# Sums of weight blocks in a seven-product up-projection: on VectorE, or by accumulating DMAs

## The chip, the core and the metric

One core of a Trainium2 chip runs the whole program. The metric is the time of one execution on the device in microseconds (us). Of the two versions the same input is computed in one launch.

## What is computed

One decoder layer over 512 tokens of width 2048, in float32: two mixer branches, an output projection, and then the part that the change is in, a gated feed-forward block of width 5632.

```python
h = rms_norm(x, ffn_norm_g[l])
gate, up = jnp.split(h @ w_up[l], 2, axis=-1)
gate = causal_depthwise_conv(gate, ffn_conv_w[l]) + ffn_conv_b[l]
x = x + (jax.nn.silu(gate) * up) @ w_down[l]
...
return rms_norm(x, final_norm_g)
```

## The kernel before

**Stages.** The program runs the mixers, the output projection, the up-projection and the down-projection one after the other on TensorE. Every float32 product is three matmuls: each operand is split into a high and a low part of type float32r, and `mm3` (line 486) adds high times high, high times low and low times high in PSUM. ScalarE casts the high part of a weight piece (`ACT.copy`), VectorE subtracts it from the raw weights and gets the low part. All instructions are recorded by one helper, so the profile gives line 97 (L97) for nearly all; tiles tell them apart.

**The up-projection.** The loop over `f` (lines 491 to 522) has 44 pairs: 128 columns of gate and 128 columns of up. The weights of a pair are four blocks of 128 x 1024 (512 KB each): block `ij` has i = 1 for gate and 2 for up, j = 1 or 2 for the two halves of the 2048 input channels. The tokens also come in two halves of 256. Eight block products would be due; a scheme of the Strassen-Winograd kind makes seven. Each is 8 steps of 3 matmuls of 256 columns, so a pair has 168 matmuls. Four of the seven weight operands are sums of blocks. The operands of the tokens, `XB` (plain halves) and `XT` (sums and differences), are made once, in `operands` (line 1272), from `h`, the tokens scaled by `ffn_g`. PSUM banks `bx`, `by`, `bz`, `bv` take the seven products, and `up_out` (line 1423) adds them up on VectorE, applies `rstd2`, the convolution, silu and the product, and stores the result to `scr_a`.

**The weights' path.** `up_products` (line 1333) is a generator that `refill` (line 1415) advances between matmuls until 6 pieces are ready ahead of TensorE. Before, SP loads blocks 11 and 22 into `raw` (3 buffers) and blocks 12 and 21 into `uraw` (3 buffers). `cast` (line 1355) makes the high part of half a block on ScalarE, `low` (line 1364) the low part on VectorE. The pieces live in two rings of 4 high and 4 low buffers (`whi`/`wlo` and `uhi`/`ulo`), so at most 8 pieces exist. `combine` (line 1369) is one VectorE instruction over 128 x 1024; `steps` (line 1375) lists the seven operands in the order in which they are made and hangs four `combine`s and the next pair's loads on them, as actions after the first or second cast of an operand. Blocks are overwritten in place: 22 becomes 22 + 21, and so on.

**Order of the work.** Every engine carries out its own instructions in program order. That order comes from `Flow` (line 102), a planner that keeps a clock for each engine (`account`, line 145) and decides between which matmuls the other engines' instructions are emitted. SP issues all loads and stores in one queue; a load that waits for its buffer holds up what is behind it. GpSimd has no work in the up-projection but one small power operation at its start (`rsqrt_pow`, line 437, called by `rms_rows`, line 577, for `rstd2`).

**The start of the stage.** The first three blocks of pair 0 (11, 22, 12) are loaded by the general plan, `up_at` in `plan_all` (line 536); block 21 of pair 0 is loaded at the first call of `up_products`.

Of the kernel before, what the change touches and what calls it, by code (L numbers as in the profile page):

```python
# [13 lines left out]
F32 = mybir.dt.float32  # L14
# [26 lines left out]
]  # L41
KH = KT // 2
PAIRS = [m for j in range(KH) for m in (j, j + KH)]
D_PRE, D_LEFT, D_RIGHT = 8, 38, 24
SPLIT_TILES = 1
BA_LAG = 3
# [55 lines left out]
class Flow:  # L102
# [42 lines left out]
    def account(self, eng, op, out, ins, kw):  # L145
        c = self.clock
        ko, ki = self.key(out), [self.key(i) for i in ins]
        start = c[eng]
        for k in ki if op == "dma_start" else ki + [ko]:
            r, e = self.ready.get(k, (0.0, None))  # L150
            start = max(start, r + self.SEM * (not (e == eng == "pe")) + 0.05 * (e == "pe" != eng))
        start = max(start, self.avail.get(ko, 0.0) + self.SEM)
        if op == "dma_start":
            size = out.nbytes if hasattr(out, "nbytes") else 0
            size = int(np.prod(out.shape)) * 4
            if eng == "pool":
                c["pool"] = go = start + 1.08
            else:
                c[eng] = start
                c["hw"] = go = max(start, c["hw"]) + 0.45  # L160
            run = size / 360e3 * (2.0 if int(out.shape[-1]) * 4 < 512 else 1.0)
            c["dma"] = max(go + 0.65, c["dma"]) + run
            end = c["dma"] + 1.0
        else:
            n = int(np.prod(out.shape[1:]))
            ni = max([n] + [int(np.prod(i.shape[1:])) for i in ins]) if op in ("tensor_reduce", "bn_stats") else n
            if eng == "pe":
                rhs = kw.get("rhs", kw.get("identity"))
                cols = int(np.prod(rhs.shape[1:]))
                floor = 0.025  # L170
                if op == "transpose":
                    rate = 2
                elif rhs.dtype == F32:
                    rate, floor = 4, int(np.prod(kw["lhsT"].shape[1:])) / 600.0
                else:
                    rate, floor = 1, (cols + 32) / 2400.0
                dur = max(cols * rate / 2400.0, floor) + (0.0025 if rate > 1 else 0.0)
                if start - c["pe"] > 0.05:
                    self.stall += start - c["pe"]
                    self.log.append((round(c["pe"], 1), round(start - c["pe"], 2), str(ko)))  # L180
            elif eng == "act":
                ps = any(k.split("_")[0] in PSUM_NAMES for k in ki if isinstance(k, str))
                aps = sum(hasattr(kw.get(a), "tensor") for a in ("scale", "bias"))
                dur = n / 1200.0 + (0.051 if ps else 0.093) + 0.093 * aps
                f = kw.get("func")
                if f in (AF.Silu, AF.Exp, AF.Sigmoid) and f != self.table:
                    self.table = f
                    dur += 1.28
            elif eng == "dve":
                ap_scalar = op == "scalar_tensor_tensor" or hasattr(kw.get("scalar1"), "tensor")  # L190
                dur = (ni + (124 if ap_scalar else 66)) / 960.0
            else:
                dur = 0.96 if kw.get("op") == ALU.pow else n * (0.0009 if op == "memset" else 0.002) + 0.03
            end = c[eng] = start + dur
        self.ready[ko] = (end, eng if op != "dma_start" else None)
        for k in ki + [ko]:
            self.last[k] = max(self.last.get(k, 0.0), end)
# [107 lines left out]
def tile_trunk(ctx: ExitStack, tc: tile.TileContext, xT, w_k, w_ba, w_m, pw, w_out, w_up, w_down, par_d, cst_d, out):  # L305
# [97 lines left out]
    def pc(n, i=0, w=1):  # L403
        return par[:, OFF[n] - KT + i : OFF[n] - KT + i + w]
# [187 lines left out]
            fl.matmul(ps2[:, blk(i)], lhsT=r[:, i : i + 1].to_broadcast([P, P]), rhs=ident)  # L592
        return r, ps2

    def rms_stats(total, bcast):
        r, ps2 = yield from rms_rows([total], range(NB))
        ACT.copy(out=bcast, in_=ps2)
        free(ps2)
        return r

# [659 lines left out]

    xpool = xctx.enter_context(tc.tile_pool(name="operands", bufs=1, reuse_waits="tile"))
    tpool = tctx.enter_context(tc.tile_pool(name="halves", bufs=1, side="right", reuse_waits="tile"))
    XT = [fl.tile(xpool, [P, 4, T], F32R, "xt", KH, nm("xt")) for _ in range(KH)]
# [6 lines left out]
    def operands(j, xa, xb):  # L1272
        h = fl.tile(tpool, [P, 2 * T], F32, "h", 2, nm("h"))
        for i, x in enumerate((xa, xb)):
            ACT.activation(out=h[:, i * T : (i + 1) * T], in_=x, func=AF.Copy, scale=pc("ffn_g", j + i * KH))
        fl.live["xv"] -= 2
        yield S(h)
        d = fl.tile(tpool, [P, 2 * T], F32, "d", 2, nm("d"))
# [1 line left out]
        ACT.copy(out=b[:, 0, 0:HT], in_=h[:, 0:HT])  # L1280
        ACT.copy(out=b[:, 1:3, 0:HT], in_=v2(h[:, T:]))
        V.tensor_tensor(
            out=v2(d[:, 0:T]), in0=h.rearrange("p (a b) -> p a b", b=T)[:, :, HT:T], in1=v2(h[:, 0:T]),
            op=ALU.subtract)
        yield S(b)
        V.tensor_tensor(out=b[:, 0, HT:T], in0=h[:, 0:HT], in1=b[:, 0, 0:HT].bitcast(F32), op=ALU.subtract)
        V.tensor_tensor(out=d[:, T : T + HT], in0=h[:, T + HT :], in1=d[:, 0:HT], op=ALU.subtract)
        V.tensor_tensor(out=b[:, 1:3, HT:T], in0=v2(h[:, T:]), in1=b[:, 1:3, 0:HT].bitcast(F32), op=ALU.subtract)
        V.tensor_tensor(out=d[:, T + HT :], in0=h[:, T : T + HT], in1=d[:, T : T + HT], op=ALU.subtract)
        yield S(d)  # L1290
        ACT.copy(out=xt[:, :, 0:HT], in_=v2(d))
        yield S(xt)
        V.tensor_tensor(out=xt[:, :, HT:T], in0=v2(d), in1=xt[:, :, 0:HT].bitcast(F32), op=ALU.subtract)

    xvs = []

    def load_xv():
# [22 lines left out]
            op_ev.append(fl.spawn(operands(i // 2, xvs[i - 1], t)))  # L1320
    rstd2 = rstd_tile("rstd2_bc")
    fl.drain(op_ev)
    fl.spawn(rms_stats(total, rstd2))
    tctx.close()
    actx.close()
    dpre = ctx.enter_context(tc.tile_pool(name="down0", bufs=1, side="right", reuse_waits="tile"))
# [6 lines left out]
    def up_products():  # L1333


        blocks = {}

        def load(f, *names):
            for n in names:
                if f == NF:  # L1340
                    if n in (11, 22):
                        up_done.append(True)
                        load_next()
                    continue
                i, j = n // 10 - 1, n % 10 - 1
                if n in (11, 22):
                    t = fl.tile(wpool, [P, 1024], F32, "raw", 3, nm("wraw"))
                else:
                    t = U("uraw", 3, 1024)
                SP.dma_start(t, w_up[2 * f + i][:, j * 1024 : (j + 1) * 1024])  # L1350
                blocks[f, n] = t

        pend = deque()

# [11 lines left out]
            V.tensor_tensor(out=lo, in0=src, in1=hi.bitcast(F32), op=ALU.subtract)  # L1366
            pieces.append((hi, lo))

        def combine(out, a, b, op=ALU.subtract):
            V.tensor_tensor(out=out, in0=a, in1=b, op=op)  # L1370

        blocks.update({(0, n): raws[up_at + i] for i, n in enumerate((11, 22, 12))})
        load(0, 21)

        def steps(f, a11, a22, a12, a21):

            def start():
                load(f + 1, 21)
                if f:
                    load(f + 1, 11)  # L1380

            def s2():
                combine(a22, a22, a11)
                load(f + 1, 22 if f else 11)

            return [
                (a11, start, None), (a22, None, lambda: combine(a22, a21, a22, ALU.add)),
                (a12, lambda: combine(a21, a11, a21), None), (a22, None, s2),
                (a21, lambda: combine(a12, a12, a22), lambda: load(f + 1, 12)),
                (a22, None, None if f else lambda: load(1, 22)), (a12, None, None)]  # L1390

        then = None
        for f in range(NF):
            units = steps(f, *[blocks.pop((f, n)) for n in (11, 22, 12, 21)])
            if f == 0:
                units[0][1]()
                units[1][2]()
                yield
                units = units[2:]
            for t, *acts in units:  # L1400
# [90 lines left out]
    for f in range(NF):  # L1491
# [2 lines left out]
        ev2, ev3, ev4 = Event(), Event(), Event()  # L1494
        if f == NF - 1:
            early = fl.spawn(act_loads(range(D_PRE // 2)))
        for n, (b, c, x) in enumerate((
                (bx, 0, [t[:, 0] for t in XB]), (bz, HT, [t[:, 3] for t in XT]), (bv, 0, [t[:, 1] for t in XB]),
                (by, 0, [t[:, 0] for t in XT]), (by, HT, [t[:, 1] for t in XT]), (bx, HT, [t[:, 2] for t in XT]),
                (bz, 0, [t[:, 2] for t in XB]))):  # L1500
            for k in range(KH):
                if k % 4 == 0:
                    hi, lo = pieces.popleft()
# [6 lines left out]
                if k % 4 == 3:  # L1510
                    for _ in step:
                        pass
            if n == 0:
                s1 = U("s1", 2, HT)
                ACT.copy(out=s1, in_=bx[:, 0:HT])
                out_ev.append(fl.spawn(up_out(f, s1, bx, by, bz, bv, ev2, ev3, ev4)))
            elif n == 2:
                fl.finish(ev2)
            elif n == 5:
                fl.finish(ev3)  # L1520
            elif n == 6:
                fl.finish(ev4)
    fl.drain([early])
    xctx.close()
# [36 lines left out]
    def down_add(m, ps, ts):  # L1561
        t = L("dt")
        V.tensor_tensor(out=t[:, ts], in0=ps, in1=rstd2[:, ts], op=ALU.mult)
        V.tensor_tensor(out=x2[m][:, ts], in0=x2[m][:, ts], in1=t[:, ts], op=ALU.add)

    def down(c, m):
        ps = mtile(View(c), (lambda k: d_free(c * FC + k)) if m == KT - 1 else None)
# [123 lines left out]
```

## Time and profile before

| What | Value |
|---|---|
| Time, median of 2 runs | 2182.1 us (2181.62 to 2182.57) |
| The profiled execution: its own time | 2180.41 us |
| The profiled execution: span of the trace | 2178.6 us |
| Mean granted TensorE clock | 0.993 of full speed |
| TensorE busy | 2156.8 us (99%) |
| VectorE busy | 1626.3 us (75%) |
| ScalarE busy | 954.9 us (44%) |
| GpSimd busy | 60.9 us (3%) |

Times inside the trace are counted from the start of the span; the execution's own time has 1.8 us more around it. PE is TensorE's matmuls and PEld its weight loads, DVE is VectorE, ACT ScalarE, POOL GpSimd, SP the engine that issues DMAs. The modelled end of a matmul overlaps the next one's start, so the pitch of matmuls is read from starts, not from the mean duration. The up-projection lies between about 782 and 1670 us.

### The profile page before, as it was taken

The page shows a single profiled execution, that of the slowest core. Times are in us where ns is not written, and L with a number is a line of the kernel's source. Part 1 is how long each engine was busy: PE and PEld are TensorE (multiplying, and loading weights), DVE is VectorE, ACT ScalarE, POOL GpSimd, SP SyncE. Part 2 cuts the span into 40 slices and gives each one's busy share as a digit, 9 for nine tenths or more (in the row PEclk, how much of TensorE's full clock was granted, in tenths as well). Part 3 has the DMA queues.
Part 4 walks back from the last instruction along what each step waited for, and adds up shares of the span by engine and source line. Part 5 has one row for each costly group of instructions (what it writes and reads, how often), then busy time and mean ns, then how long its engine had stood idle before and what let it go on. Part 6 is the DMA issues. An engine that isn't in the chain of part 4 may idle for free.

```text
span 2178.6 us, 34210 instructions
## 1 busy us (share of the span) xinstructions
PE 2156.8 (99%) x13340; PEld 1924.6 (88%) x13340; DVE 1626.3 (75%) x2684; ACT 954.9 (44%) x1664; POOL 60.9 (3%) x59
## 2 busy tenths in 40 slices
PE   9999999999999999999999999999999999999997
PEld 7888888888888889999999999999998888888886
DVE  6899778888843789999999999999998533343344
ACT  5643544443423554545454555545555322233231
POOL 0310011000000000000000000000000000000000
PEclk9999999999999999999999999999999999999998
DMA  5252433333563534333433343343345533343333
GB/s 197 91 161 90 124 97 112 111 97 126 189 198 116 190 130 131 118 111 122 131 112 115 124 128 109 113 131 117 112 122 198 191 111 117 106 134 92 99 96 110
DMA packets 116754, 276.63 MB, mean 127 GB/s; under 512 B 23280, under 2 KB 35952, under 8 KB 116592
## 3 DMA queue, kind: packets, MB, share of 16 engines
q1 hardware_dynamic: 116448, 274.45, 39.7%
q8 instruction: 104, 1.70, 0.3%
q14 instruction: 58, 0.48, 0.1%
q10 hardware_dynamic: 144, 0.01, 0.0%
HBM read 240.33 MB, written 34.08 MB: 126 GB/s over the span
## 4 chain that ended last, share of the span: by engine, by line
PE 98%; DVE 1%; issue 0%; DMA 0%; ACT 0%; SPq 0%; POOL 0%; POOLq 0%; DVEq 0%; ACTq 0%
PE acc L97 53%; PE bz L97 12%; PE by L97 12%; PE bx L97 11%; PE bv L97 6%; PE tr L97 1%; PE e L97 1%; PE pv L97 0%; PE ba L97 0%; PE po L97 0%; PE y L97 0%; PE psn L97 0%; PE pk L97 0%; PE pq L97 0%; DVE x L97 0%
## 5 line engine op out<-in xcount | busy, mean ns | idle before, releaser
L97 DVE TENSOR_TENSOR wlo<-wraw,whi 128x512 fp32r<-128x512 f32 (+1 forms) x616 | 414.6, 677 | 330.1 <-ACT whi L97 328.0
L97 ACT CAST whi<-wraw 128x512 fp32r<-128x512 f32 (+1 forms) x616 | 370.0, 606 | 611.7 <-PE acc L97 453.1
L97 PE MATMUL acc<-dh,whi 128*128 128x512 f32 (+1 forms) x726 | 280.8, 387 | 4.0 <-ACT dh L97 4.0
L97 PE MATMUL acc<-dl,whi 128*128 128x512 f32 (+1 forms) x726 | 280.6, 386 | 0.0
L97 PE MATMUL acc<-dh,wlo 128*128 128x512 f32 (+1 forms) x726 | 280.4, 386 | 0.0
L97 PE MATMUL acc<-xgh,whi 128*128 128x512 f32 x640 | 262.6, 410 | 0.1
L97 PE MATMUL acc<-xgl,whi 128*128 128x512 f32 x640 | 252.5, 395 | 0.5 <-DVE xgl L97 0.5
L97 PE MATMUL acc<-xgh,wlo 128*128 128x512 f32 x640 | 252.7, 395 | 0.0
L97 DVE SCALAR_TENSOR_TENSOR cacc<-u,par,cacc 128x495 f32<-128x495 f32 (+22 forms) x240 | 172.5, 737 | 1.8 <-ACT cacc L97 0.4
L97 PEld LDWEIGHTS acc<-dh,whi 128*128 128x128 f32 x726 | 136.9, 189 | 33.2 <-ACT dh L97 4.5
L97 PEld LDWEIGHTS acc<-dl,whi 128*128 128x128 f32 x726 | 136.9, 189 | 29.3 <-DVE dl L97 0.4
L97 PEld LDWEIGHTS acc<-dh,wlo 128*128 128x128 f32 x726 | 136.9, 189 | 28.8
L97 ACT CAST uhi<-wraw 128x512 fp32r<-128x512 f32 x176 | 109.3, 621 | 105.1 <-PE by L97 68.0
L97 ACT CAST whi<-uraw 128x512 fp32r<-128x512 f32 x130 | 80.9, 622 | 151.7 <-DVE uraw L97 82.6
L97 PEld LDWEIGHTS acc<-xgh,wlo 128*128 128x128 f32 x640 | 120.3, 188 | 28.4
L97 DVE TENSOR_TENSOR ulo<-wraw,uhi 128x512 fp32r<-128x512 f32 x176 | 120.7, 686 | 31.4 <-ACT uhi L97 31.4
L97 PEld LDWEIGHTS acc<-xgl,whi 128*128 128x128 f32 x640 | 120.7, 189 | 25.7 <-DVE xgl L97 1.2
L97 PEld LDWEIGHTS acc<-xgh,whi 128*128 128x128 f32 x640 | 120.6, 188 | 25.7 <-ACT xgh L97 0.9
L97 PE MATMUL by<-xt,whi 128*128 128x256 f32 x704 | 129.6, 282 | 0.0
L97 PE MATMUL by<-xt,uhi 128*128 128x256 f32 x704 | 129.0, 280 | 0.0
L97 PEld LDWEIGHTS by<-xt,whi 128*128 128x128 f32 x704 | 108.7, 190 | 0.0
L97 PEld LDWEIGHTS by<-xt,uhi 128*128 128x128 f32 x704 | 108.5, 188 | 0.0
(277 smaller groups left out, 4710.6 us busy)
## 6 DMA issues: line engine op xcount, KB each, us to landing
wraw<-in_w_up_dram SPq DMA_DIRECT2D x89, 512.0 KB, 4.5
uraw<-in_w_up_dram SPq DMA_DIRECT2D x87, 512.0 KB, 4.4
wraw<-in_w_m_dram SPq DMA_DIRECT2D x74, 512.0 KB, 3.6
wraw<-in_w_down_dram SPq DMA_DIRECT2D x64, 512.0 KB, 3.6
wraw<-in_w_out_dram SPq DMA_DIRECT2D x32, 512.0 KB, 3.6
wraw<-in_w_down_dram SPq DMA_DIRECT2D x32, 384.0 KB, 3.3
scr_a<-fa SPq DMA_DIRECT2D x44, 256.0 KB, 2.1
dl<-scr_a SPq DMA_DIRECT2D x44, 256.0 KB, 5.4
```

Source lines behind the costliest of these rows:

```text
L97: return f(**kw) if not args else f(out, *args, **{k: v for k, v in kw.items() if k != "out"})
```

## The change

The four `combine`s go. Two new tags take the place of `uraw`, of the same size together: `us` (2 buffers) and `u3` (1 buffer). `pair` has SP load one block into such a buffer (22 into `us`, 11 into `u3`) and GpSimd issue a DMA that adds block 21 from HBM to it (`accum_op=ALU.add`). The operand s1 is `us` at that point; after its two low parts are made, a further accumulating DMA adds block 11 to the same buffer, which then is s2, and another adds block 12, which gives s4. `u3` is s3. Block 12 now goes to `raw`. So a pair has five plain loads and four accumulating DMAs of 512 KB each. The order of the products is a table, `PRODUCTS`: for the first pair 11, 22, s1, 12, s2, s3, s4, for all others s1, 11, 22, s2, 12, s3, s4. To make all sums additions, the tokens' operands are made with other signs: `h` is scaled by -`ffn_g`, two of the differences in `operands` become `scalar_tensor_tensor`, `rstd2` is negated, and `down_add` subtracts. The planner's account lets an accumulating DMA wait for its destination.

```diff
+PRODUCTS = [["11", "22", "s1", "12", "s2", "s3", "s4"], ["s1", "11", "22", "s2", "12", "s3", "s4"]]
...
-        for k in ki if op == "dma_start" else ki + [ko]:
+        for k in ki if op == "dma_start" and "accum_op" not in kw else ki + [ko]:
...
-    def rms_stats(total, bcast):
+    def rms_stats(total, bcast, sign=1.0):
         r, ps2 = yield from rms_rows([total], range(NB))
-        ACT.copy(out=bcast, in_=ps2)
+        ACT.activation(out=bcast, in_=ps2, func=AF.Copy, scale=sign)
...
-            ACT.activation(out=h[:, i * T : (i + 1) * T], in_=x, func=AF.Copy, scale=pc("ffn_g", j + i * KH))
+            ACT.activation(out=h[:, i * T : (i + 1) * T], in_=x, func=AF.Copy, scale=neg_g[:, j + i * KH : j + i * KH + 1])
...
-            out=v2(d[:, 0:T]), in0=h.rearrange("p (a b) -> p a b", b=T)[:, :, HT:T], in1=v2(h[:, 0:T]),
+            out=v2(d[:, 0:T]), in0=v2(h)[:, 0::3, :], in1=h[:, HT:T].unsqueeze(1).to_broadcast([P, 2, HT]),
...
-        V.tensor_tensor(out=d[:, T : T + HT], in0=h[:, T + HT :], in1=d[:, 0:HT], op=ALU.subtract)
+        V.scalar_tensor_tensor(
+            out=d[:, T : T + HT], in0=h[:, T + HT :], scalar=-1.0, in1=d[:, 0:HT], op0=ALU.mult, op1=ALU.subtract)
...
+    V.tensor_scalar(out=neg_g, in0=pc("ffn_g", 0, KT), scalar1=-1.0, scalar2=0.0, op0=ALU.mult, op1=ALU.add)
...
+        def add(t, f, n):
+            POOL.dma_start(t, block(f, n), accum_op=ALU.add)
+
+        def pair(f, tag, bufs, n):
+            if f < NF:
+                blocks[f, tag] = t = U(tag, bufs, 1024)
+                SP.dma_start(t, block(f, n))
+                add(t, f, 21)
...
-            return [
-                (a11, start, None), (a22, None, lambda: combine(a22, a21, a22, ALU.add)),
-                (a12, lambda: combine(a21, a11, a21), None), (a22, None, s2),
-                (a21, lambda: combine(a12, a12, a22), lambda: load(f + 1, 12)),
-                (a22, None, None if f else lambda: load(1, 22)), (a12, None, None)]
+        pair(0, "us", 2, 22)
+        pair(0, "u3", 1, 11)
+        def steps(f):
+            a11, a22, a12, us, u3 = [blocks.pop((f, n)) for n in (11, 22, 12, "us", "u3")]
+            units = {
+                "s1": (us, lambda: pair(f + 1, "us", 2, 22), lambda: add(us, f, 11)),
+                "11": (a11, None, lambda: load(f + 1, 11)), "22": (a22, None, lambda: load(f + 1, 22)),
+                "s2": (us, None, lambda: add(us, f, 12)), "12": (a12, None, lambda: load(f + 1, 12)),
+                "s3": (u3, None, lambda: pair(f + 1, "u3", 1, 11)), "s4": (us, None, None)}
+            return [units[n] for n in PRODUCTS[f > 0]]
...
-        V.tensor_tensor(out=x2[m][:, ts], in0=x2[m][:, ts], in1=t[:, ts], op=ALU.add)
+        V.tensor_tensor(out=x2[m][:, ts], in0=x2[m][:, ts], in1=t[:, ts], op=ALU.subtract)
```

In `steps`, an entry is the buffer, the action after the first cast and the action after the second. An action is emitted after the next cast and after the low part of the cast that it belongs to.

## Rows read from the trace of the kernel before

**Rows 1.** The page: busy time of each engine, and the chain by line.
```profile
PE 2156.8 (99%) x13340; PEld 1924.6 (88%) x13340; DVE 1626.3 (75%) x2684; ACT 954.9 (44%) x1664; POOL 60.9 (3%) x59
...
PE 98%; DVE 1%; issue 0%; DMA 0%; ACT 0%; SPq 0%; POOL 0%; POOLq 0%; DVEq 0%; ACTq 0%
```
**Rows 2.** Stretches: start, body and end of the up-projection, then the down-projection.
```profile
core 0: us, PE busy (x) PEld busy (x) DVE busy (x) ACT busy (x) POOL busy (x), PEclk, DMA share, GB/s
...
868.00:1667.00 799.00, 799.00 (x6723) 799.00 (x6722) 738.87 (x1080) 404.11 (x682) 0.00 (x0) 1.00 0.38 119
1667.00:1680.00 13.00, 8.97 (x45) 7.18 (x45) 9.95 (x16) 5.66 (x10) 0.00 (x0) 0.81 0.74 260
...
781.50:797.00 15.50, 12.08 (x67) 11.58 (x66) 12.94 (x19) 7.97 (x15) 1.38 (x1) 0.67 0.27 86
```
**Rows 3.** The chain in order of time (start, us, what): one pair later.
```profile
1199.29 5.71 PE by L97 x48
1219.27 5.71 PE by L97 x48
```
**Rows 4.** Groups by form, 1100 to 1800: sums, low parts, casts, a scaled sum.
```profile
L97 DVE TENSOR_TENSOR wraw<-wraw,wraw 128x1024 f32<-128x1024 f32 x28 | 34.3, 1225 | 1.0
L97 DVE TENSOR_TENSOR wraw<-uraw,wraw 128x1024 f32<-128x1024 f32 x28 | 34.3, 1224 | 1.0
L97 DVE TENSOR_TENSOR uraw<-uraw,wraw 128x1024 f32<-128x1024 f32 x28 | 34.1, 1218 | 0.0
L97 DVE TENSOR_TENSOR uraw<-wraw,uraw 128x1024 f32<-128x1024 f32 x28 | 34.1, 1217 | 0.0
...
L97 DVE TENSOR_TENSOR wlo<-wraw,whi 128x512 fp32r<-128x512 f32 x157 | 107.6, 686 | 55.3 <-ACT whi L97 55.3
L97 ACT CAST whi<-wraw 128x512 fp32r<-128x512 f32 x157 | 97.4, 622 | 145.9 <-PE acc L97 55.8 <-DVE wraw L97 27.6 <-PE bz L97 26.1
...
L97 DVE SCALAR_TENSOR_TENSOR fa<-fg,par,fa 128x511 f32<-128x511 f32 x29 | 21.6, 744 | 0.3 <-ACT fa L97 0.3
```
**Rows 5.** Waits, 1100 to 1800: us in total, times, longest us.
```profile
ACT whi L97 <- DVE uraw L97: 54.0, 28, 2.6
ACT whi L97 <- PE bx L97: 46.5, 56, 2.2
ACT uhi L97 <- PE by L97: 44.8, 56, 0.8
```
**Rows 6.** DMA issues (us to landing): 868 to 1667, then at 1199.4 and 1223.1.
```profile
uraw<-in_w_up_dram SPq DMA_DIRECT2D x77, 512.0 KB, 4.5
...
uraw<-in_w_up_dram SPq DMA_DIRECT2D x1, 512.0 KB, 3.2
...
wraw<-in_w_up_dram SPq DMA_DIRECT2D x1, 512.0 KB, 5.8
```
**Rows 7.** Stretch in the down-projection where loads stand in line.
```profile
1680.00:1690.00 10.00, 10.00 (x42) 8.19 (x41) 9.82 (x18) 9.08 (x17) 0.00 (x0) 0.91 1.05 392
```
**Rows 8.** Timeline of SP: one issue alone.
```profile
1219.43 0.33 SPq L97 DMA_DIRECT2D uraw<-in_w_up_dram  x1
```
**Rows 9.** The page's DMA queues, and GpSimd's one instruction of this stage.
```profile
q1 hardware_dynamic: 116448, 274.45, 39.7%
q8 instruction: 104, 1.70, 0.3%
q14 instruction: 58, 0.48, 0.1%
q10 hardware_dynamic: 144, 0.01, 0.0%
...
789.59 1.38 POOL L97 TENSOR_TENSOR rstd<-ms,mhalf 128x4 f32<-128x4 f32 x1 [186.09 <-DVE ms L97]
```
**Rows 10.** Timeline of the start: first loads of the stage, and the third product.
```profile
782.81 2.09 SPq L97 DMA_DIRECT2D uraw<-in_w_up_dram  x2
...
796.80 0.40 PE L97 MATMUL bv<-xb,whi 128*128 128x256 f32 x2
```

More of the change, by code (lines that the diff above doesn't have):

```diff
@@ L1286, in operands @@
         V.tensor_tensor(out=b[:, 0, HT:T], in0=h[:, 0:HT], in1=b[:, 0, 0:HT].bitcast(F32), op=ALU.subtract)
-        V.tensor_tensor(out=d[:, T : T + HT], in0=h[:, T + HT :], in1=d[:, 0:HT], op=ALU.subtract)
+        V.scalar_tensor_tensor(
+            out=d[:, T : T + HT], in0=h[:, T + HT :], scalar=-1.0, in1=d[:, 0:HT], op0=ALU.mult, op1=ALU.subtract)
         V.tensor_tensor(out=b[:, 1:3, HT:T], in0=v2(h[:, T:]), in1=b[:, 1:3, 0:HT].bitcast(F32), op=ALU.subtract)
-        V.tensor_tensor(out=d[:, T + HT :], in0=h[:, T : T + HT], in1=d[:, T : T + HT], op=ALU.subtract)
+        V.scalar_tensor_tensor(
+            out=d[:, T + HT :], in0=h[:, T : T + HT], scalar=-1.0, in1=d[:, T : T + HT], op0=ALU.mult,
+            op1=ALU.subtract)
         yield S(d)
@@ L1322, in tile_trunk @@
     fl.drain(op_ev)
-    fl.spawn(rms_stats(total, rstd2))
+    fl.spawn(rms_stats(total, rstd2, -1.0))
     tctx.close()
@@ L1333, in up_products, with block, load @@
     def up_products():
+        def block(f, n):
+            i, j = n // 10 - 1, n % 10 - 1
+            return w_up[2 * f + i][:, j * 1024 : (j + 1) * 1024]
         blocks = {}
[L1338 to L1351, printed above, removed]
+        def load(f, n):
+            if f < NF:
+                blocks[f, n] = t = fl.tile(wpool, [P, 1024], F32, "raw", 3, nm("wraw"))
+                SP.dma_start(t, block(f, n))
+            elif n != 12:
+                up_done.append(True)
+                load_next()
+        def add(t, f, n):
+            POOL.dma_start(t, block(f, n), accum_op=ALU.add)
+        def pair(f, tag, bufs, n):
+            if f < NF:
+                blocks[f, tag] = t = U(tag, bufs, 1024)
+                SP.dma_start(t, block(f, n))
+                add(t, f, 21)
         pend = deque()
@@ L1367, in low @@
             pieces.append((hi, lo))
-        def combine(out, a, b, op=ALU.subtract):
-            V.tensor_tensor(out=out, in0=a, in1=b, op=op)
         blocks.update({(0, n): raws[up_at + i] for i, n in enumerate((11, 22, 12))})
[L1373 to L1384, printed above, removed]
-            return [
-                (a11, start, None), (a22, None, lambda: combine(a22, a21, a22, ALU.add)),
-                (a12, lambda: combine(a21, a11, a21), None), (a22, None, s2),
-                (a21, lambda: combine(a12, a12, a22), lambda: load(f + 1, 12)),
-                (a22, None, None if f else lambda: load(1, 22)), (a12, None, None)]
+        pair(0, "us", 2, 22)
[8 more added lines that the diff above has]
+            return [units[n] for n in PRODUCTS[f > 0]]
         then = None
         for f in range(NF):
-            units = steps(f, *[blocks.pop((f, n)) for n in (11, 22, 12, 21)])
+            units = steps(f)
             if f == 0:
-                units[0][1]()
-                units[1][2]()
+                for _, _, act in units[:2]:
+                    act()
                 yield
@@ L1496, in tile_trunk @@
             early = fl.spawn(act_loads(range(D_PRE // 2)))
[L1497 to L1500, printed above, removed]
+        products = {
+            "s1": (by, 0, [t[:, 0] for t in XT]), "11": (bx, 0, [t[:, 0] for t in XB]),
+            "22": (bz, HT, [t[:, 3] for t in XT]), "s2": (bx, HT, [t[:, 2] for t in XT]),
+            "12": (bv, 0, [t[:, 1] for t in XB]), "s3": (by, HT, [t[:, 1] for t in XT]),
+            "s4": (bz, 0, [t[:, 2] for t in XB])}
+        for n, w in enumerate(PRODUCTS[f > 0]):
+            b, c, x = products[w]
             for k in range(KH):
@@ L1512, in tile_trunk @@
                         pass
-            if n == 0:
+            if w == "11":
                 s1 = U("s1", 2, HT)
@@ L1516, in tile_trunk @@
                 out_ev.append(fl.spawn(up_out(f, s1, bx, by, bz, bv, ev2, ev3, ev4)))
-            elif n == 2:
+            elif w == "12":
                 fl.finish(ev2)
-            elif n == 5:
+            elif w == "s3":
                 fl.finish(ev3)
-            elif n == 6:
+            elif w == "s4":
                 fl.finish(ev4)
```

1 line of the change is left out of this document (added).

## The prediction

> **What bounds the kernel now.** I read the page first. TensorE is busy 99% of the span, and the chain of work that ended last is 98% PE [rows 1]; everything else can only cost time by making TensorE wait. Then the stretches: in the body of the up-projection TensorE is busy for all 799.00 of 799.00 us at a granted clock of 1.00, while VectorE works 738.87 us (92%), ScalarE 404.11 and GpSimd nothing [rows 2]. The reader should see that VectorE's 92% is no bound: not one idle microsecond of TensorE stands beside it. The chain gives the period: the same piece begins at 1199.29 and at 1219.27, so a pair takes 19.97 us for 168 matmuls, 0.119 us each [rows 3]. The waits show why VectorE's load does no harm. ScalarE does wait for VectorE's sums, up to 2.6 us at a time, but about as often its casts wait for TensorE to give back a piece buffer [rows 5]. The weights' path runs up to 8 pieces ahead, and a pair has 14, so there are up to some 8 x 19.97 / 14 = 11 us in store. Idle time exists only at the two ends of the stage: 3.4 us of 15.5 at the start (there at a granted clock of 0.67) and 4.0 us of 13 at the end (0.81) [rows 2].
>
> **What goes.** Four VectorE sums per pair, 1.22 us each [rows 4]: 4.9 us per pair, 44 x 4.9 = 215 us of busy time. It all lies beside TensorE at 100%, so it is worth nothing in the body. At the ends it could give back at most the 3.4 + 4.0 us of idle time; I count 0, since at the start TensorE waits for the statistics' chain and at the end for activations that come back from HBM, and neither goes through a sum.
>
> **What is added, small parts.** The negated copy of the gains is one small instruction; 16 `scalar_tensor_tensor` in place of `tensor_tensor` cost by the nearest rows (744 ns at 511 columns against 686 at 512 [rows 4]) under 0.1 us each, beside the matmuls of the stage before. The other sign changes keep count and shape. Together 0; uncovered they would be 1.5 us.
>
> **What is added, DMA.** Per pair 5 plain loads and 4 accumulating DMAs of 512 KB take the place of 4 loads. No row shows an accumulating DMA: all queues of before are hardware ones or instruction fetch [rows 9]. So bounds. A plain 512 KB at the best rate seen, 392 GB/s with the engines at a share of 1.05 [rows 7], takes 524 KB / 392 = 1.34 us on the 16 engines. An accumulate reads the destination as well as the source; if both reads share what carries one now, it is 2 x 1.34 = 2.7 us; if the second read is hidden, 1.34. I take 2.7, because nothing shows that the engines read two streams at the rate of one, and keep both. Load on the engines: 5 loads and half a store, 5.5 x 1.34 = 7.4 us, plus 4 x 1.34 = 5.4 or 4 x 2.7 = 10.8: 12.8 or 18.2 us of every 19.97. They would still fit, the second barely.
>
> The Trainium skill ("Collectives: The Full Stack", The bandwidth ceiling) says that an adding DMA is limited by its two reads and runs at half the rate of a copy. By that rule the value is 2.7 us, not 1.34; no run here has shown it yet.
>
> **What is added, waits: the loop.** This decides. The sums s1, s2 and s4 are made in one buffer one after the other, and GpSimd issues in program order: it has to add block 21 to the *next* pair's buffer before it adds block 11 to this one, and that buffer's plain load can start only when s4 of the pair before has been split. So there is a loop that must close within one pair. From the landing of s2:
>
> - two casts (0.62 each) and the last low part (0.69) [rows 4], with the hand-overs: 2.0 us;
> - GpSimd issues the add of block 12. No row has the price: below it is SP's 0.33 for a plain issue [rows 8], above it GpSimd's 1.38 for a small instruction [rows 9]. I take 1.0, nearer to the same engine's row;
> - its transfer: a load alone lands 3.2 us after its issue [rows 6]; less 0.33 and 1.34 leaves 1.5 us that are no transfer. 1.5 + 2.7 = 4.2 us;
> - casts and low part of s4: 2.0 us;
> - SP loads block 22 into the freed buffer: 4.5 us, the median of the stage, between 3.2 alone and 5.8 beside another load [rows 6];
> - GpSimd issues the adds of 21 and then of 11; both go through the same engines, and the second issue is covered by the first transfer: 1.0 + 1.5 + 2 x 2.7 = 7.9 us, and s2 of the next pair has landed.
>
> Sum 2.0 + 1.0 + 4.2 + 2.0 + 4.5 + 7.9 = 21.6 us, 1.6 more than the 19.97 that TensorE needs. The store of pieces does not help against a loop that is longer than the period: it is used up in a few pairs and never refilled. Behind GpSimd's waits stand only its own adds. On ScalarE the cast of s2 holds up those of 12, s3 and s4 behind it, and TensorE waits for these. The loop closes 43 times: 43 x 1.63 = 70 us.
>
> **Start of the stage.** In pair 0 the third product began at 796.80 [rows 10]. Now it is s1: its load (issued at 782.81 [rows 10], landed by 787 to 789) is ready, but GpSimd's add stands behind the power operation, which ends at 790.97 [rows 9]; 1.0 + 4.2 us later is 796.2, and cast and low part make it 797.5. With similar delays of 1 to 2 us at s2 and s4, where no store of pieces exists yet, I add 4 us (0 to 8).
>
> **Sum.** 2180.4 us (the profiled execution) + 70 + 4 - 0 = 2254.4; the median lies 1.7 us above that execution: 2256 us. With a load of 3.2 us and issues of 0.33 the loop takes 19.0 us and nothing is lost; with 5.8 and 1.38 it takes 23.7: 43 x 3.7 = 160, 2346 us. A measurement of this kernel can tell about 2% from no change, that is 2226 us, so the forecast's own range is 2226 to 2346.
>
> **Rivals.**
>
> *A: the loop fits, and nothing is gained (not slower).* Place: the accumulate's transfer, which counts three times in the loop. At 1.34 us it is 21.6 - 3 x 1.36 = 17.5 us, below 19.97, and the store of pieces stays filled. It decides at (19.97 - 17.5) / 3 + 1.34 = 2.2 us per accumulate. For it: only 12.8 of 19.97 us of the engines are then used, and each landing before s2 and s4 may be 8 pieces late before TensorE notices. Against it: no row shows a DMA that reads twice at the price of one. Time: 2182 + 4 = 2186.
>
> *B: the accumulate is much dearer than two copies.* At 4 us the loop takes 17.5 + 3 x 2.66 = 25.5 us and the engines carry 7.4 + 16 = 23.4: 43 x 5.5 = 237, 2422 us. The same happens if TensorE's waits bring its clock down as at the start of the stage, where it fell to 0.67 beside 3.4 us of idle time [rows 2]. For it: pieces of the loop share the engines with five plain loads. Against it: a dearer accumulate needs a reason beyond the second read.
>
> *C: VectorE's freedom pays.* This needs idle time of TensorE that a sum causes. Even all idle time of both ends, 7.4 us, is 0.3%: 2175.
>
> **How the numbers follow.** The forecast gets 0.46, A 0.42, B 0.11, C 0.01. Slower by over 2%: 0.46 + 0.11 = 0.57; within 2%: 0.42; faster: 0.01. The single point on which forecast and A part is whether the accumulate costs more than 2.2 us; between 1.34 and 2.7 that is a little nearer to the upper end than to an even chance. The range goes from 2178 (A with a few us gained at the ends) to 2370; what it leaves out is most of B and C.
>
> **What would show it.** Right: in the body TensorE idles about 1.6 us per pair, just before the first matmul of s2 or s4; ScalarE's casts of `us` wait for GpSimd's DMAs; an accumulating DMA lands 5 us or more after its issue; the period is 21 to 23 us; VectorE's busy time falls by some 215 us; DMA share in the body is above 0.8. Wrong: a period of 19.97 with TensorE at 100%, which is A; or waits at other operands, a granted clock below 1.00 in the body, or a DMA share of 1, which is B. HBM reads must rise by 44 x 5 x 0.524 = 115 MB in any case; if not, the change does not do what it says.

## The result, and the profile after

The changed kernel takes **2553.6 us** (median of 2 runs, 2549.92 to 2557.25) against 2182.1 before: a ratio of **1.1704**, 95% interval 1.1685 to 1.1722. It is slower, as forecast, but by 371 us where 74 were forecast, and the time lies 184 us above the upper end of the range. The profiled execution took 2557.25 us.

The page of the profile after: busy time of the engines, the queues (packets, MB, share of 16 engines' span), the chain by engine, the DMA issues of the weights.
```profile
span 2555.4 us, 34697 instructions
...
PE 2244.5 (88%) x13340; PEld 2013.4 (79%) x13340; DVE 1420.8 (56%) x2509; ACT 923.2 (36%) x1664; POOL 216.2 (8%) x235
...
q1 hardware_dynamic: 122784, 297.52, 34.7%
q0 software_dynamic: 25344, 92.29, 20.8%
...
HBM read 355.68 MB, written 34.08 MB: 153 GB/s over the span
...
PE 51%; DMA 35%; DVE 5%; ACT 4%; issue 4%; POOL 1%; ACTq 0%; POOLq 0%; SPq 0%; DVEq 0%
...
wraw<-in_w_up_dram SPq DMA_DIRECT2D x132, 512.0 KB, 5.7
us<-in_w_up_dram POOLq DMA_DIRECT2D x132, 512.0 KB, 7.8
...
us<-in_w_up_dram SPq DMA_DIRECT2D x44, 512.0 KB, 6.5
u<-in_w_up_dram SPq DMA_DIRECT2D x44, 512.0 KB, 5.3
u<-in_w_up_dram POOLq DMA_DIRECT2D x44, 512.0 KB, 7.2
```
(The tile `u3` stands as `u`, and the helper's line is now L98.) The chain that was 98% PE [rows 1] is 51% PE and 35% DMA. VectorE does 205.5 us less work, as the change intends, and its share fell to 56%: the engine that was relieved was never what the end waited for. A queue that did not exist before [rows 9], q0, carries the 176 accumulating DMAs.

The stretch of the body after; columns as in [rows 2]:
```profile
870.00:2040.00 1170.00, 906.56 (x6866) 898.42 (x6865) 562.51 (x935) 379.13 (x690) 143.15 (x162) 0.86 0.71 174
```
TensorE, idle for nothing in the body before [rows 2], is now idle for 263 of 1170 us, at a granted clock of 0.86. No engine is full: DMA 0.71, VectorE 0.48, GpSimd 0.12. When everything has idle time and the work still does not come faster, look for a loop of waits. The waits say where it is held (1000 to 1900; us in total, times, longest):
```profile
ACT whi L98 <- DMA us<-in_w_up_dram: 552.7, 63, 16.5
...
POOL us L98 <- DVE ulo L98: 377.5, 35, 13.9
...
PE bx L98 <- ACT s L98: 209.1, 32, 9.4
```
ScalarE waits for the accumulating DMAs, GpSimd for the low parts, and TensorE only for a small copy of ScalarE, `s`. That copy is not slow; ScalarE's timeline (start, us, what, idle time before and its releaser) shows that it stands behind the cast of s2, which waits 12.52 us for its DMA:
```profile
1342.41 0.62 ACT L98 CAST whi<-us 128x512 fp32r<-128x512 f32 x1 [12.52 <-DMA us<-in_w_up_dram]
...
1345.72 0.36 ACT L98 COPY s<-bx 128x256 f32<-128x256 f32 x1
```

**The loop, measured.** The chain of waits gives one turn of it without a gap (start, us, what):
```profile
1297.69 6.60 DMA us<-in_w_up_dram
...
1304.85 0.54 POOL us L98
1305.40 8.84 DMA us<-in_w_up_dram
...
1314.34 0.63 ACT whi L98
...
1316.57 5.49 DMA us<-in_w_up_dram
...
1322.16 0.63 ACT whi L98
...
1323.42 0.76 DVE fa L98
...
1324.87 0.70 DVE ulo L98
1325.58 6.50 DMA us<-in_w_up_dram
...
1333.28 9.04 DMA us<-in_w_up_dram
```
From load to load it takes 1325.58 - 1297.69 = 27.9 us:

| Step of the loop | Predicted | From the chain |
|---|---|---|
| load of 22 lands | 4.5 | 6.6 |
| adds of 21 and 11 issued and landed | 7.9 | 10.0 (1304.29 to 1314.26) |
| s2: casts, low parts | 2.0 | 2.3 (to 1316.57) |
| add of 12 issued and landed | 5.2 | 5.5 (to 1322.08) |
| s4: casts, low parts | 2.0 | 3.5 (to 1325.58) |
| sum | 21.6 | 27.9 |

On the average the turn is a little longer. SP's loads of `us`, one a pair, in a view of that tile (1000 to 1900; min/median/max ns, first and last start):
```profile
L98 SPq DMA_DIRECT2D us<-in_w_up_dram x31: 327/328/328, 1011.3 to 1873.2; - x31
```
That is 861.9 / 30 = 28.7 us a pair, against 19.97 [rows 3]. 43 x 8.76 = 377 us is nearly the whole loss. From its first matmul to the first of the next stage the up-projection takes 383 us more (773.7 to 2045.0 us against 781.5 to 1669.9), so that some 6 us are left for its ends; the stages ahead of it take 8 us less (b1 and b2 look into it) and the last one 2 us more. The periods below are read in the same way, between 1000 and 1600.

GpSimd's queue shows what lies beside the loop:
```profile
1316.57 0.89 POOL L98 DMA_DIRECT2D us<-in_w_up_dram  x1 [9.93 <-DVE ulo L98]
1324.97 0.88 POOL L98 DMA_DIRECT2D u<-in_w_up_dram  x1 [7.51 <-DVE fa L98]
1332.64 1.78 POOL L98 DMA_DIRECT2D us<-in_w_up_dram  x2 [6.79 <-DVE g L98]
```
The add of 21 to s3's buffer goes out at 1324.97, 0.6 us before the load of 22: the two share the engines. At 1332.64 the adds of 21 (next pair) and 11 (this pair) go out together. So the add that this pair's s2 needs stands behind an add for the next pair, and that one can't go out before the next pair's load of 22 has landed.

### The profile page after: what moved, and what is told of

It reads as the page before. It is cut to its first block, busy times and chain, and to the rows that moved or that the text cites. A ratio compares the mean times of both kernels' runs of the same rounds, so it can differ in the third digit from the quotient of the medians.

```text
span 2555.4 us, 34697 instructions
## 1 busy us (share of the span) xinstructions
PE 2244.5 (88%) x13340; PEld 2013.4 (79%) x13340; DVE 1420.8 (56%) x2509; ACT 923.2 (36%) x1664; POOL 216.2 (8%) x235
## 3 DMA queue, kind: packets, MB, share of 16 engines
q0 software_dynamic: 25344, 92.29, 20.8%
HBM read 355.68 MB, written 34.08 MB: 153 GB/s over the span
## 4 chain that ended last, share of the span: by engine, by line
PE 51%; DMA 35%; DVE 5%; ACT 4%; issue 4%; POOL 1%; ACTq 0%; POOLq 0%; SPq 0%; DVEq 0%
PE acc L98 43%; DMA us<-in_w_up_dram 34%; ACT whi L98 3%; PE bx L98 2%; DVE ulo L98 2%; DVE wlo L98 1%; ACT uhi L98 1%; POOL us L98 1%; PE tr L98 1%; DVE cacc L98 1%; DVE fa L98 1%; PE bv L98 0%; PE e L98 0%; PE by L98 0%; PE bz L98 0%
## 5 line engine op out<-in xcount | busy, mean ns | idle before, releaser
L98 DVE TENSOR_TENSOR wlo<-wraw,whi 128x512 fp32r<-128x512 f32 (+1 forms) x570 | 382.6, 675 | 316.7 <-ACT whi L98 315.0
L98 ACT CAST whi<-wraw 128x512 fp32r<-128x512 f32 (+1 forms) x570 | 341.3, 604 | 520.4 <-PE acc L98 443.0
L98 DVE TENSOR_TENSOR wlo<-us,whi 128x512 fp32r<-128x512 f32 x132 | 91.1, 690 | 624.5 <-ACT whi L98 617.1
L98 PE MATMUL bx<-xt,whi 128*128 128x256 f32 x352 | 115.7, 429 | 277.6 <-ACT s L98 277.6
L98 ACT CAST whi<-us 128x512 fp32r<-128x512 f32 x132 | 81.7, 619 | 768.3 <-DMA us<-in_w_up_dram 764.4
L98 PEld LDWEIGHTS bx<-xt,whi 128*128 128x128 f32 x352 | 92.0, 319 | 286.3 <-ACT s L98 286.3
L98 PE MATMUL acc<-dh,whi 128*128 128x512 f32 (+1 forms) x726 | 281.2, 387 | 8.4 <-ACT dh L98 8.4
L98 PE MATMUL acc<-dh,wlo 128*128 128x512 f32 (+1 forms) x726 | 279.9, 386 | 0.0
L98 PE MATMUL acc<-dl,whi 128*128 128x512 f32 (+1 forms) x726 | 278.5, 384 | 0.0
L98 PE MATMUL acc<-xgh,whi 128*128 128x512 f32 x640 | 261.3, 408 | 1.0 <-ACT xgh L98 1.0
L98 PE MATMUL acc<-xgh,wlo 128*128 128x512 f32 x640 | 251.1, 392 | 0.0
L98 PE MATMUL acc<-xgl,whi 128*128 128x512 f32 x640 | 250.2, 391 | 0.3 <-DVE xgl L98 0.3
L98 POOL DMA_DIRECT2D us<-in_w_up_dram x132 | 117.0, 975 | 752.4 <-DVE ulo L98 493.1
L98 DVE SCALAR_TENSOR_TENSOR cacc<-u,par,cacc 128x495 f32<-128x495 f32 (+22 forms) x240 | 173.6, 742 | 1.7 <-ACT cacc L98 0.3
L98 PEld LDWEIGHTS acc<-dh,whi 128*128 128x128 f32 x726 | 136.9, 189 | 35.6 <-ACT dh L98 8.9
L98 PEld LDWEIGHTS acc<-dh,wlo 128*128 128x128 f32 x726 | 136.7, 188 | 29.1
L98 PEld LDWEIGHTS acc<-dl,whi 128*128 128x128 f32 x726 | 136.8, 188 | 28.7 <-DVE dl L98 0.4
L98 PEld LDWEIGHTS acc<-xgh,wlo 128*128 128x128 f32 x640 | 120.2, 188 | 27.2
L98 PEld LDWEIGHTS acc<-xgh,whi 128*128 128x128 f32 x640 | 120.5, 188 | 24.3 <-ACT xgh L98 1.7
L98 PEld LDWEIGHTS acc<-xgl,whi 128*128 128x128 f32 x640 | 120.6, 188 | 23.8 <-DVE xgl L98 0.9
L98 PE MATMUL by<-xt,whi 128*128 128x256 f32 x704 | 131.8, 285 | 2.5 <-ACT whi L98 2.5
L98 PE MATMUL by<-xt,uhi 128*128 128x256 f32 x704 | 129.5, 283 | 0.0
```

The source lines that it names most:

```text
L98: return f(**kw) if not args else f(out, *args, **{k: v for k, v in kw.items() if k != "out"})
```

## The experiments

e2, e4, e6, e7 and e9 are single executions; the others are medians of four or more.

**e1, the order of GpSimd's queue.** Three theories were open: a loop through the order of GpSimd's adds, a shortage of the DMA engines, and the price of the accumulate. The edit puts the add of 11 ahead of the next pair's load and add.
```diff
-"s1": (us, lambda: pair(f + 1, "us", 2, 22), lambda: add(us, f, 11)),
+"s1": (us, None, lambda: (add(us, f, 11), pair(f + 1, "us", 2, 22))),
```


> One edit in the changed kernel: after s1 is split, GpSimd first adds block 11 to this pair's buffer, and only then comes the next pair's load of block 22 and its add of 21. Theory (a loop of waits of 28.05 us per pair, closed by GpSimd's program order): the load of 22 and the add of 21 leave the loop; what is left from s1's split to the next one is two adds of some 5.8 us and three times casts and low part, 18 to 21 us, so the period is 20 to 21.5 us and the time 2190 to 2260 us. Rival (the 16 DMA engines cannot carry two-read accumulates, whatever their order): the bytes are the same, the period stays at 26 us or more, the time above 2450 us.

Measured: 2332.5 us, ratio 1.0694 (1.0678 to 1.0710), period 23.4 us. One line of order, with the same DMAs, gives back 221 of the 371 us: the order is the larger part, and the rival, a shortage of the engines whatever the order, does not hold for it. It misses the expected 2260 by 72 us. Its chain shows a second head of the queue of the same kind:
```profile
1206.18 3.92 DMA u<-in_w_up_dram
...
1210.66 0.54 POOL u L98
1211.20 13.35 DMA us<-in_w_up_dram
```
The add for s3 waits for its own load and stands ahead of the add of 11.

**e2, the same DMAs without the addition.** GpSimd's four DMAs per pair as plain copies.
```diff
-            POOL.dma_start(t, block(f, n), accum_op=ALU.add)
+            POOL.dma_start(t, block(f, n))
```


> One edit in the changed kernel: GpSimd's four DMAs per pair are plain copies into the same buffers, so the sums are left out (each buffer holds the block that was copied last). Theory: the order of the loop is the same, each of GpSimd's transfers moves half as much, three transfers in the loop lose about 1.5 us each and the load beside them 1 to 2 us: 28.05 - 6 = 22 us, time 2290 us (2230 to 2360). If the price of an accumulate were not its second read but GpSimd's issue or its completion, the period would stay near 28 us and the time near 2550.

Measured: 2278.2 us, period 22.4 us. The queues of its page:
```profile
q1 hardware_dynamic: 122784, 297.52, 39.1%
q0 software_dynamic: 25344, 92.29, 12.2%
```
Packets and bytes are those of after. q0 holds the engines for 12.2% of 2276.4 us / 176 = 1.58 us per copy, and in after for 20.8% of 2555.4 / 176 = 3.02 us per accumulate: 1.9 times. GpSimd's issue is shorter too, 0.54 us in place of 0.88, so the 6.3 us by which the period falls are not the transfers' alone. And with copies at the price of copies the period is still 2.4 us longer than TensorE's. So the dear accumulate adds to a period that is too long without it.

**e3, VectorE's sums in the new order.** All signs, buffers and the order of the products as in after, but five plain loads and VectorE's additions; nothing on GpSimd.
```diff
+        def plus(t, b):
+            V.tensor_tensor(out=t, in0=t, in1=b, op=ALU.add)
...
+            def s1():
+                plus(u3, a11)
+                pair(f + 1, "us", 2, 21)
```


> The changed kernel with its signs, its product order and its buffers, but the four sums made by VectorE with an addition each, from plain loads (five per pair). Theory: nothing but the DMAs costs time; period 19.97 us, time 2178 to 2190 us. If the new order of products or the wait of TensorE for ScalarE's copy of bx had a part in the loss, the time would stay above 2226 us.

Measured: 2198.7 us, ratio 1.0082 (1.0066 to 1.0099): 9 us above what was expected, and far from after. Its waits name the reason (1000 to 1600):
```profile
DVE u L98 <- DMA u<-in_w_up_dram: 51.7, 29, 2.3
```
VectorE's sum for s3 waits in VectorE's queue for its load, ahead of other work. This is the mechanism of e1 on another engine; e8 takes it up.

**e4, one accumulate less.** Only s3 is summed by VectorE.
```diff
-                add(t, f, 21)
+                if tag == "us":
+                    add(t, f, 21)
...
-        pair(0, "u3", 1, 11)
+        pair(0, "u3", 1, 21)
```


> The changed kernel with s3 alone made by VectorE (block 21 loaded plainly, block 11 added there): three accumulating DMAs per pair. Theory: the load of 22 in the loop no longer stands beside the add of s3 and lands after 4 us, not 6.5: period 25.5 us, time 2445 us (2400 to 2480). Rival (the engines' work of 19.9 us per pair is what counts): it falls by 3.0 us or 15%, the period with it to 23.8, time 2370 us.

Measured: 2453.7 us, period 26.3 us: 2.4 us less a pair, somewhat under one accumulate's 3.0, and as the theory said. The load of 22 lands after 4.5 us (median, 870 to 1850) where it took 6.6 beside s3's add. The head of the queue is still there: the add of 11 goes out behind the one that waits for this load.

**e5, both: the order of e1, and s3 by VectorE,** a product later.
```diff
-                "s1": (us, None, lambda: (add(us, f, 11), pair(f + 1, "us", 2, 22))),
-                "11": (a11, None, lambda: load(f + 1, 11)), ...
+                "s1": (us, s1, s2),
+                "11": (a11, None, lambda: (plus(u3, a11), load(f + 1, 11))), ...
```
(the diff is against e1; `s2` holds the add of 11 and then the `pair`, and `s1` adds only for the first pair)

> The changed kernel with both edits together: GpSimd adds block 11 to this pair's buffer before the next pair's load and add, and s3 is made by VectorE (a plain load of 21 and one addition, late enough that the load has landed). Three accumulating DMAs per pair, nothing of s3 in GpSimd's queue. Theory (waits in a loop): what is left in the loop is two adds of 6 to 8 us and casts and low parts, 19 to 21 us, so the period is 20 to 21 us and the time 2182 to 2240 us. If the adds are late for another reason than their neighbours in GpSimd's queue and on the engines, the period stays near the 23.4 us of the run with the order alone, 2330 us.

Measured: 2182.2 us (median of 10), ratio 1.0006 (0.9997 to 1.0016): no difference from before, with three accumulating DMAs per pair and a period of 19.97 us. A stretch of its body:
```profile
1000.00:1600.00 600.00, 600.00 (x5049) 600.00 (x5048) 457.94 (x722) 301.67 (x511) 78.94 (x91) 1.00 0.86 224
```
TensorE is at 600.00 of 600 and a clock of 1.00 while the DMA engines are at 0.86, more than after's 0.71. So neither this traffic nor three accumulates as such hold up TensorE; e4 and e5 have the same DMAs and lie 271 us apart. They differ in GpSimd's order and in the place of s3's sum, which is worth 29 us in e3 and e8. The fourth accumulate is put back in e10. That e5 equals before is a balance: its up-projection takes 11 us longer (776.0 to 1675.3 against 781.5 to 1669.9) and the other stages 9 us less, a gain that e8 and b1 have too. Against e8, which has VectorE's sums and is else alike, e5 is 12 us slower. Some 6 us lie at the start: between 797 and 870 TensorE works for 67.15 of 73 us in e5 and for all in before and e8.

**e6, a third buffer for `us`,** so that the load of the next pair need not wait for s4. It fits by making a pool of the next stage smaller.
```diff
-D_PRE, D_LEFT, D_RIGHT = 8, 38, 24
+D_PRE, D_LEFT, D_RIGHT = 6, 38, 24
...
-        pair(0, "us", 2, 22)
+        pair(0, "us", 3, 22)
...
-                "s1": (us, lambda: pair(f + 1, "us", 2, 22), lambda: add(us, f, 11)),
+                "s1": (us, lambda: pair(f + 1, "us", 3, 22), lambda: add(us, f, 11)),
```


> The changed kernel with three buffers for s1, s2 and s4 in place of two (two of the eight tiles for early activations are given up for the room), GpSimd's order as in the changed kernel. Theory: the next pair's load of 22 no longer waits until s4 of the pair before is split, so 6.5 us of load leave the loop, and the add of 21 can be moving while s4 is awaited: period 20 to 23 us, time 2190 to 2310 us. Rival (only the order of GpSimd's adds counts, the load does not): little changes, above 2480 us. If it ends near the 2330 us of the run with the order alone, both have come upon the same next bound, the 16 engines with four accumulates and five loads.

Measured: 2425.9 us, period 25.8 us. The theory missed, and so did its rival, which said above 2480 us: the buffer is a part of the cause, and not the larger one. GpSimd's timeline shows what remains:
```profile
1221.14 0.87 POOL L98 DMA_DIRECT2D u<-in_w_up_dram  x1 [7.62 <-DVE fa L98]
1222.67 1.77 POOL L98 DMA_DIRECT2D us<-in_w_up_dram  x2 [0.66 <-issue]
```
The load is out of the loop now, so the three adds go out in one row: s3's, the next pair's and, last, the one that s2 of this pair waits for. In this kernel's chain it lands 12.22 us later. The load was worth about 3 us of the loop; the order is worth more.

**e7, less work for TensorE.** The period could also be long because TensorE's clock fell to 0.86. This kernel leaves out one of the three matmuls of each step of the up-projection.
```diff
-                mm3(
-                    b[:, c : c + HT], hi[:, sl], lo[:, sl], x[k][:, 0:HT], x[k][:, HT:T],
-                    k == 0, k == KH - 1)
+                fl.matmul(b[:, c : c + HT], lhsT=hi[:, sl], rhs=x[k][:, 0:HT], start=k == 0, stop=False)
+                fl.matmul(b[:, c : c + HT], lhsT=lo[:, sl], rhs=x[k][:, 0:HT], start=False, stop=k == KH - 1)
```


> The changed kernel with one of the three matmuls of each product step of the up-projection left out (high weights times low tokens): TensorE's work per pair falls from 19.97 to 13.3 us. Theory: TensorE, its lower clock and its wait for ScalarE's copy of bx are no part of the loop, so the period stays at 28 us and the time within 2530 to 2560 us. Rival (TensorE at the lower clock is part of what sets the period): the time falls below 2480 us.

Measured: 2532.8 us, period 28.2 us. The same stretch of its body:
```profile
1000.00:1600.00 600.00, 332.07 (x2370) 327.77 (x2370) 293.16 (x489) 192.98 (x365) 74.92 (x85) 0.75 0.72 176
```
With a third of the matmuls gone and a clock of 0.75, the period changes by 0.5 us. TensorE and its clock are not in the loop: in after the lower clock is paid out of idle time.

**e8, e3 with s3's sum one product later.**
```diff
             def s1():
-                plus(u3, a11)
+                if f == 0:
+                    plus(u3, a11)
...
-                "11": (a11, None, lambda: load(f + 1, 11)), ...
+                "11": (a11, None, lambda: (plus(u3, a11), load(f + 1, 11))), ...
```


> Signs, order and buffers of the changed kernel with all four sums on VectorE, as in the run before it, but VectorE adds block 11 to s3's buffer one product later, when the load of 21 has landed. Theory: the 0.8% of that run was VectorE's wait for this load (2.3 us at the longest), not the signs and not the order of the products: period 19.97 us, time 2178 to 2188 us. If signs or order cost something, 2190 us or more remain.

Measured: 2169.8 us, ratio 0.9945 (0.9928 to 0.9961). In the body TensorE works for 790.00 of 790.00 us: e3's wait was the cause of the 29 us between the two. That it is faster than before by 12 us was not expected; b1 and b2 look for it.

**e9, the add of 21 to `us` left out.** The rival to e1's reading: it is not the place of the add of 21 but that there is one more.
```diff
-                add(t, f, 21)
+                if tag == "u3":
+                    add(t, f, 21)
```


> The changed kernel without the add of block 21 to the buffer of s1, s2 and s4 (block 21 is left out of these three sums; s3 keeps its add): three accumulating DMAs per pair, as in the run in which VectorE made s3, but the one that stands in GpSimd's queue ahead of this pair's add of 11 is gone. Theory: GpSimd no longer waits for the next pair's load before it adds 11, the loop is open, what is left is two adds and casts as in the run with the order alone, less the add of 21 in the same line: period 20 to 22 us, time 2180 to 2270 us. Rival (the number of accumulates and their work on the engines decides): the same as with s3 on VectorE, 2454 us.

Measured: 2333.5 us, period 23.8 us, neither of the two expected. It has three accumulates per pair as e4 and is 120 us faster, so their number does not decide, and it equals e1, which has all four: with the add of 21 out of the way, whether moved or gone, the time is the same. What is left is again s3's add with its load ahead of the add of 11 (in the chain 4.41 us for the load of `u` and then 13.32 for the add).

**b1 and b2, a spare tile.** The change adds a 64-byte tile per partition, `neg_g`, to the pool of constants. b1 is the kernel before with such a tile, written once and not used; b2 has 128 bytes.
```diff
+    spare = cpool.tile([P, 16], F32, name="spare")
+    V.memset(spare, 0.0)
```


> The kernel before with a spare tile of 64 bytes per partition (as large as the negated gains) in the pool of constants, written once and not read. In all kernels with the negated gains the 512-column matmuls of the early stages follow each other in 228.9 ns, in the kernel before in 232.4 ns, although TensorE's instructions are the same there. Theory: the tile moves the addresses of what is allocated after it, and that is the cause: 228.9 ns, time 2168 to 2174 us. Rival (signs, order or the lighter VectorE give the 12 us of the run with all sums on VectorE): 232.4 ns and 2181 us.

> The same with a spare tile of 128 bytes. If any move of the addresses helps, or the tile's presence as such, it takes the same time as with 64 bytes, about 2170 us. If it is the position within a block of 128 bytes, it is back at 232.4 ns and 2181 us.

Measured: 2169.6 us (0.9951, 0.9936 to 0.9966) and 2170.8 (0.9951, 0.9935 to 0.9968). So a tile of the size of `neg_g` is by itself worth the 12 us of e8, and the change gained from it by accident. The chain of the stage before the up-projection, in before and then in b1:
```profile
608.75 172.91 PE acc L97 x744
```
```profile
602.42 170.33 PE acc L97 x744
```
232.4 ns for each of these matmuls of 512 columns becomes 228.9 in b1. In b2's chain it is 226.7 (168.68 us for 744), in after's 228.9 (164.83 for 720).

**e10, all four accumulates in the best order found.** Every load is issued some 7 us or more ahead of its add (that of `u` at 1222.00, its add at 1229.60), and GpSimd's order is add 11, 21 to s3, 12, 21 to the next pair's `us`.
```diff
+            def s1():
+                add(us, f, 11)
+                add(u3, f, 21)
+
+            def s2():
+                add(us, f, 12)
+                if f + 1 < NF:
+                    add(blocks[f + 1, "us"], f + 1, 21)
```


> The changed kernel with all four accumulating DMAs, same bytes, two buffers, but in an order in which GpSimd never stands before a load that has just been issued: add 11 to s1's buffer, add 21 to s3's buffer (loaded in the pair before), add 12 to s2's buffer, add 21 to the next pair's buffer (loaded half a pair before). Theory (what costs the time is GpSimd's queue: adds for the next pair that wait for their loads, ahead of the add that this pair waits for): the period falls from 28 us to 20 to 22 us, the time to 2185 to 2275 us; the engines' work of about 19.9 us per pair is then the next bound, so 19.97 us is hardly reached. Rival (four accumulates are more than the engines carry beside five loads, in any order): no better than the run with the order alone, 23.4 us and 2330 us.

Measured: 2270.7 us, ratio 1.0401 (1.0382 to 1.0419), period 21.9 us.
```profile
1000.00:1600.00 600.00, 563.91 (x4585) 559.02 (x4584) 380.89 (x627) 252.78 (x465) 95.89 (x108) 0.97 0.90 228
```
283 of the 371 us are back. What is left is again a loop of waits. From this kernel's chain (start, us, what):
```profile
1215.18 0.54 POOL us L98
1215.73 11.01 DMA us<-in_w_up_dram
...
1226.78 2.27 issue
...
1229.06 5.99 DMA us<-in_w_up_dram
...
1235.09 2.29 issue
...
1237.40 0.54 POOL us L98
```
One turn takes 22.2 us. The add of 21 for the next pair goes out right behind the add of 12 and lands 11.0 us later; s1 is split (2.3 us; the chain says issue, but the casts and low parts of `us` lie in it); the add of 11 lands after 6.0; s2 is split (2.3), and only then do the next two adds go out. The DMA engines are at 0.90: 0.90 x 21.9 = 19.7 us of transfers per pair, which would be 99% of a period of 19.97, so they have next to no slack either. How much of the last 88 us is this order and how much the engines' load, no run separates. Of all the kernels run none with an accumulating DMA beats before; e8 and b1 do, and both keep VectorE's sums.

## Why the prediction was right in direction and wrong in size

- **What bounds, what goes: right.** VectorE's 215 us (205.5 measured) were worth nothing, as TensorE at 799.00 of 799.00 [rows 2] said. HBM reads rose by 115 MB to 355.68.
- **The loop: right.** The prediction named its members and its order: the next pair's add of 21 ahead of this pair's add of 11, the load behind s4. The chain has these transfers and no others, and e1 and e9, which take that add out of the way, return 220 us.
- **The price of an accumulate: nearly right, and not the decisive point.** 2.7 us of the engines were taken, 3.0 measured, against 1.58 for a copy, which had been put at 1.34. The Trainium skill ("Collectives: The Full Stack", The bandwidth ceiling) says of ReduceScatter, a collective that adds, that the two reads of the add make it half as fast as one that copies. The trace agrees for this kernel's DMAs, with 3.02 against 1.58 us. But the prediction let the forecast and rival A part at this price, with 17.5 us for the loop at a copy's price. e2 has a copy's price, and its period is 22.4.
- **The step that failed: the sum of 21.6 us.** The transfers' durations came from rows of before, whose DMA engines are at 0.38 in the body [rows 2]; in after they are at 0.71, and the loop's operations run beside those of the same pair that are not in it. The three terms that were mis-sized: *the load of 22*, 4.5 predicted, the median of the stage [rows 6], and 6.6 measured, above the 5.8 taken as the upper end, because s3's add goes out 0.6 us ahead of it (without that add it is 4.5, e4); *the two adds*, 7.9 and 10.0, most likely since plain loads go through the engines with them (from 1333.3 to 1335.0 the loads' queue q1 fills 94.5% of the engines' time and the adds' q0 2.4%); *the work of s4*, 2.0 and 3.5, since two scaled sums of 0.76 us stand ahead of the last low part in VectorE's queue. These are 5.7 of the 6.3 us that were missing, times 43. s3's add was not in the sum, neither as a transfer nor as a place in the queue, of which the prediction only said that "behind GpSimd's waits stand only its own adds": e4 shows it at 2.4 us a pair, and e1 as the next head of the queue.
- **Rival A: too generous.** That nothing is lost had 0.42, on the ground that a cheap accumulate brings the loop down to 17.5 us. By e2 even a copy's price does not bring the period down to 19.97. The forecast's own load on the engines, 18.2 of 19.97 us, left little room for transfers that don't overlap; it is 19.7 in e10.
- **Rival B: its size without its reason.** Its loop of 25.5 us and its 2422 us came nearer than the forecast, by luck: an accumulate takes 3.0 us of the engines and not 4, and the lower clock, its other reason, is ruled out by e7.
- **The signs.** Waits of `us` casts for GpSimd's DMAs, landings above 5 us: as predicted. TensorE's idle time is in front of s2's first matmul (`bx`, behind the copy `s`), as predicted, but 209.1 us in 900, some 6.7 us a pair in place of 1.6. The DMA share is 0.71, not above 0.8: the predicted load spread over a longer period. The clock of 0.86 was listed as a sign of B; e7 shows that it does not set the period.
- **The start.** 4 us were predicted. Between 797 and 870 TensorE works for 56.98 of 73 us where it worked for all before; the loop starts with the first pair, so this is not the start alone. In e5, whose body is not held up, it is 67.15 of 73: some 6 us.

## What to carry to other kernels

An engine that issues DMAs in program order is a queue: never put a transfer that waits for a fresh load ahead of one that current work waits for; here that order alone was worth 221 of 371 us. Write down the loop from a buffer's release to its next use with every transfer that is in flight at the same time, not with durations measured alone, and count an accumulating DMA as two copies (1.9 here). Work that another engine does beside a TensorE that is never idle costs no time, as VectorE's sums before, so moving it elsewhere has no time to win.

## What the runs showed that was not expected

A spare tile of 64 or 128 bytes per partition in the pool of constants, used by no instruction but its own fill, makes matmuls of 512 columns start every 228.9 ns (64 bytes) or 226.7 ns (128 bytes) in place of 232.4, and the whole kernel some 12 us faster. The tiles behind it lie at other addresses; whether it is this, and of which operand, was not settled. It means that a change of 0.5% in such a kernel can come from an added tile alone, and that a kernel with an added tile is to be compared with one that has a tile of that size and nothing else.

An accumulating DMA lands later when others were issued just ahead of it: 5.5 us after the issue for one alone in the queue (1316.57), 9.0 for the second of two (1333.28), 12.2 for the last of three (e6). Its place is not all that counts: in e9 the second of two took 13.3.
